# A fused attention block on one core: last projections a step earlier, gate scale four steps later, and an uneven last half block with its normalisation partly on TensorE

## The chip, the core and the metric

The kernel runs on one core of one Trainium2 chip. A core has five engines with queues of their own: TensorE (matmuls; PE in the profile, its weight loads PEld), VectorE (DVE), ScalarE (ACT), GpSimd (POOL), and SyncE (SP), which here only issues transfers. Sixteen DMA engines move the data. The metric is device microseconds for one execution; lower is better.

## The reference

One encoder layer over 1,024 tokens of width 1,024, in float32. One projection makes the inputs of two groups of eight heads of 64. Group A is attention in an 8 x 16 neighbourhood of a 16 x 64 token grid with a learned bias; group B is attention in a band of 128 tokens to each side with rotary positions and a learned sink. Each group's output is multiplied by SiLU of its gate columns; both are joined, projected, added to the scaled input and normalised by row.

```
h = x @ w_in
q_a, k_a, v_a, z_a, q_b, k_b, v_b, z_b = split(h)
y_a = neighborhood_attention(q_a, k_a, v_a, rel_bias)
y_b = windowed_gqa_with_sink(rotary(q_b), rotary(k_b), v_b, sink)
mixed = concat([y_a * silu(z_a), y_b * silu(z_b)])
x = layer_norm(alpha * x + mixed @ w_out) * gain + bias
```

## The kernel before

**Precision.** Large products are done as three float16 matmuls: each operand is split into a high and a low part (`xh`/`xl`, `wh`/`wl`), and high x high, high x low and low x high are added up in PSUM. So a 128-column slice of weights against 512 tokens takes 8 x 3 = 24 matmuls, and a whole projection 48.

**Stages.** First come the values, the scales and six projections. Then follows a loop over steps, written in an order by hand: `units` holds 128 attention units (64 of group B, then 64 of group A, 16 to a pair of heads). At step i, unit i's scores are made (`stage_qk`, L818 and L819, in one of four `s` banks of PSUM), DVE adds the bias and takes the row's extreme (L828), ACT takes the exponential (L844); one step later ACT and DVE split the probabilities into high and low halves (`stage_tr`, L854 and L855), which frees the bank, and SP issues the DMA that transposes them (L858). Every fourth step `stage_pv` (L883) multiplies a quad of four units, split and sent off some steps before, with the values, one unit after the other; quad q is done at step 9 + 4q up to q = 29. `stage_ot` (L903, L912) transposes finished heads and multiplies in the gate.

**Filling.** Between these, `pump_to` issues matmuls of the remaining fifteen projections: project k of `FILL` is spread evenly between `FILL_AT[k]` and `FILL_AT[k + 1]`, so the list sets how many fill matmuls (L398) each step gets. The last four projections are z2, k3, q3 and z3: a gate, the key and the query of the last pair of heads (units 112 to 127), and the last gate. From step 121 on the fill is output projection (L1031). A finished projection is taken out of PSUM by ACT and DVE (for q3 L274 and L280, in two halves of the tokens); group A's keys are also copied by POOL (L312). Weight splits, loads of bias (L786), values (L742) and output weights (L969) are put into queues for ACT, DVE, POOL and SP, and a step takes a few from each. What a step needs at once is forced out by `need`. All transfers but a few go through SP, in program order, so a transfer waits for those ahead of it.

**Gate scale.** `m_scale(0)` to `m_scale(7)` work out one scale for the gated outputs: a matmul (`z_sum`, L644), then thirteen small DVE operations (L648 to L694), one piece a step from step 2 on. Its results are read by `stage_ot`, first at step 21.

**The end.** `final` does the output projection in blocks of 128 tokens (t) and 512 columns (a), then `residual` (L1080, and statistics L1081) and `norm`. The last block's second half is done as two pieces of 256 columns, `out_mms(7, 1, ps, EO, c)`, so that the statistics of the first run under the matmuls of the second. `norm_last(7)` then normalises in three column ranges: two on DVE (256 and 608 columns), one on ACT and POOL (160), and stores each.

Of the kernel before, what the change touches and what calls it, by code (L numbers as in the profile page):

```python
# [7 lines left out]
F32 = mybir.dt.float32  # L8
# [4 lines left out]
AF = mybir.ActivationFunctionType  # L13
ALU = mybir.AluOpType

S = 1024
D = 1024
# [4 lines left out]
ALPHA = 2.0 ** 0.25  # L22
# [12 lines left out]
DSUM = (4, 7)  # L35
NR = 8
FILL = ORDER[NPRO:]
FILL_AT = [0, 8, 17, 25, 33, 41, 49, 57, 66, 74, 81, 89, 97, 105, 112, 121, 123.5, 126, 128, 131, 136]
ZTAG = {"z3": "zv", "zb3": "zc", "z2": "zs", "zb1": "zd", "zb2": "ze"}
X1AT = 4  # L40
Z3_END = 119
# [6 lines left out]
WO_POST = (7, 8)  # L48
WO_MAX = 72
EO = (4, 5, 6, 7, 0, 1, 2, 3)  # L50
WO_AT = [80, 84, 88, 92, 128, 129, 130, 131]
WO_LD = [18, 22, 26, 30, 36, 39, 42, 45, 48, 112, 116, 33, 130, 130]
WIN0 = (0, 8, 24, 40)
# [9 lines left out]
def hybrid_block(ctx, tc, xT, x, wt, wv, wo, bias, sink, gain, lbias, cos, sin, bmask, out):  # L63
    nc = tc.nc
# [10 lines left out]
    def bank(tag):  # L75
        bufs = {"pj": 2, "s": 4, "t": 2}[tag]
        return (ps1 if bufs == 1 else ps2).tile([128, 512], F32, tag=tag, name=f"ps_{tag}", bufs=bufs)
# [13 lines left out]
    for half in range(2):  # L91
        for k in range(KT):
            t = big_tile(f"x{half}{k}")
# [7 lines left out]
    identf = const.tile([128, 128], F32, name="identf")  # L101
# [328 lines left out]
    with ExitStack() as vctx:  # L430
# [5 lines left out]
        ps = bank("t")  # L436
# [140 lines left out]
        for i in range(8):  # L577
# [5 lines left out]
            ps = bank(tags[i])  # L583
# [434 lines left out]
    Q30 = LP + 3 + 4 * (len(units) // 4 - 2)  # L1018
    NU = len(units)
    def out_mms(t, a, ps, es, c=None):  # L1020
        w = 512 if c is None else 256
        o = 0 if c is None else 256 * c
        ts, cs = slice(128 * t, 128 * t + 128), slice(o, o + w)
        ps = ps[:, o:o + w]
        for e in es:
            n = WO_SEQ.index((e, a))
            if n in wo_ops:
                need(wo_ops[n], *m_ops.get(e, ()))
            woh, wol = wo_parts[n]
            for i, (lh, rh) in enumerate(((mh[e], woh), (mh[e], wol), (ml[e], woh))):  # L1030
                nc.tensor.matmul(ps, lh[:, ts], rh[:, cs],  # L1031
                                 start=(e == EO[0] and i == 0), stop=(e == EO[-1] and i == 2))
                yield
# [14 lines left out]
    def final():  # L1048
        actx.close()
        fp = ctx.enter_context(tc.tile_pool(name="fp", bufs=2, reuse_waits="tile"))  # L1050
        eps = fp.tile([128, 1], F32, name="eps", bufs=1)
        nc.vector.memset(eps, EPS)
        tiles["fp"] = fp
        for e in EO[4:]:
            m_alloc(e, fp)
        for n in range(8, 14):
            nc.gpsimd.tensor_scalar(wo_raw[n], wo_raw[n], wos, 1.0, op0=ALU.mult, op1=ALU.mult)
        for e in EO[4:]:
            m_split(e, slice(0, 512), nc.scalar.copy, nc.vector.tensor_sub)
            for n in (WO_SEQ.index((e, 0)), WO_SEQ.index((e, 1))):  # L1060
                wo_split(n)
        for e in EO[4:]:
            m_split(e, slice(512, S), nc.scalar.copy, nc.vector.tensor_sub)
        gb, bb = gain_tile[0], zslot("bb")
        nc.sync.dma_start(bb, lbias.partition_broadcast(128))
        xrs, stats = {}, {}

        def x_load(t):
            if t < 8:
                xrs[t] = fp.tile([128, D], F32, tag="xr", name="xr", bufs=NX)  # L1070
                nc.sync.dma_start(xrs[t], x[t])

        def residual(t, a, ps, c=None):
            if a == 0:
                stats[t] = fp.tile([128, 4, 6], F32, tag="stats", name="stats")
            for k in range(2) if t == 7 and c is None else (c,):
                w = 512 if k is None else 256
                o = 0 if k is None else 256 * k
                xv = xrs[t][:, 512 * a + o:512 * a + o + w]
                nc.vector.scalar_tensor_tensor(xv, ps[:, o:o + w], oinv, xv, op0=ALU.mult, op1=ALU.add)  # L1080
                nc.vector.bn_stats(stats[t][:, a if k is None else 2 * a + k, :], xv)  # L1081

        def row_stats(t):
            mv = fp.tile([128, 2], F32, tag="mv", name="mv")
            nc.vector.bn_aggr(mv, stats[t][:, :4 if t == 7 else 2, :])
            sd = fp.tile([128, 1], F32, tag="sd", name="sd")
            nc.scalar.activation(sd, mv[:, 1:2], AF.Sqrt, bias=eps, scale=ALPHA ** 2)
            return mv, sd

        def row_scale(mv, sd):  # L1090
            rstd = fp.tile([128, 1], F32, tag="rstd", name="rstd")
            nc.vector.reciprocal(rstd, sd)
            nc.vector.tensor_scalar_mul(rstd, rstd, ALPHA)
            nmr = fp.tile([128, 1], F32, tag="nmr", name="nmr")
            nc.vector.scalar_tensor_tensor(nmr, mv[:, 0:1], -1.0, rstd, op0=ALU.mult, op1=ALU.mult)
            return rstd, nmr

        def norm_last(t):
            ts = slice(128 * t, 128 * t + 128)
            xr = xrs[t]  # L1100
            mv, sd = row_stats(t)
            h0, h1, h2 = slice(0, 256), slice(256, 864), slice(864, 1024)
            nc.vector.scalar_tensor_tensor(xr[:, h0], xr[:, h0], mv[:, 0:1], gb[:, h0], op0=ALU.subtract, op1=ALU.mult)
            rstd, nmr = row_scale(mv, sd)
            nc.scalar.activation(xr[:, h2], xr[:, h2], AF.Identity, bias=nmr, scale=rstd)
            nc.vector.scalar_tensor_tensor(xr[:, h1], xr[:, h1], mv[:, 0:1], gb[:, h1], op0=ALU.subtract, op1=ALU.mult)
            nc.gpsimd.tensor_mul(xr[:, h2], xr[:, h2], gb[:, h2])
            nc.gpsimd.tensor_add(xr[:, h2], xr[:, h2], bb[:, h2])
            for h, q in ((h1, nc.sync), (h0, nc.scalar)):
                nc.vector.scalar_tensor_tensor(xr[:, h], xr[:, h], rstd, bb[:, h], op0=ALU.mult, op1=ALU.add)  # L1110
                q.dma_start(out[ts, h], xr[:, h])
            nc.sync.dma_start(out[ts, h2], xr[:, h2])

        def norm(t):
            ts = slice(128 * t, 128 * t + 128)
            xr = xrs[t]
            mv, sd = row_stats(t)
            h0, h1 = slice(0, 512), slice(512, 1024)
            nc.vector.scalar_tensor_tensor(xr[:, h0], xr[:, h0], mv[:, 0:1], gb[:, h0], op0=ALU.subtract, op1=ALU.mult)
            rstd, nmr = row_scale(mv, sd)  # L1120
            nc.scalar.activation(xr[:, h1], xr[:, h1], AF.Identity, bias=nmr, scale=rstd)  # L1121
            nc.vector.scalar_tensor_tensor(xr[:, h0], xr[:, h0], rstd, bb[:, h0], op0=ALU.mult, op1=ALU.add)
            nc.sync.dma_start(out[ts, h0], xr[:, h0])
            nc.gpsimd.tensor_mul(xr[:, h1], xr[:, h1], gb[:, h1])  # L1124
            nc.gpsimd.tensor_add(xr[:, h1], xr[:, h1], bb[:, h1])
            nc.sync.dma_start(out[ts, h1], xr[:, h1])

        for t in range(NX):
            x_load(t)
        def finish(t, a, ps):  # L1130
            residual(t, a, ps)
            halves.setdefault(t, set()).add(a)
            for n in range(normed[0], t + 1):
                if n < 7 and len(halves.get(n, ())) == 2:
                    norm(n)
                    x_load(n + NX)
                    normed[0] += 1

        halves, normed = {}, [0]
        for t, tag in ((0, "t"), (1, "t"), (2, "s")):  # L1140
            obank[t, 1] = bank(tag)
            list(out_mms(t, 1, obank[t, 1], EO[:4]))
        for e in EO[4:]:
            for t, a in sorted(obank):
                list(out_mms(t, a, obank[t, a], [e]))
                if e == EO[-1]:
                    finish(t, a, obank[t, a])
        tags = iter(("pj", "t", "pj", "t", "s", "s", "s", "s"))
        for t, a in ((3, 1), (4, 1), (5, 0), (5, 1), (6, 0), (6, 1)):
            ps = bank(next(tags))  # L1150
            list(out_mms(t, a, ps, EO))
            finish(t, a, ps)
        ps = bank(next(tags))
        list(out_mms(7, 0, ps, EO))
        residual(7, 0, ps)
        for c in range(2):
            ps = bank(next(tags) if c == 0 else "pj")
            list(out_mms(7, 1, ps, EO, c))
            residual(7, 1, ps, c)
        with tc.manual_schedule():  # L1160
            norm_last(7)
# [12 lines left out]
    for i in range(-LD, NU + LO):  # L1174
# [5 lines left out]
        per, h = divmod(i, 16)  # L1180
# [31 lines left out]
        q, m = divmod(i - LP - 3, 4)  # L1212
        if i >= Q30 + 2:
            q, m = (NU // 4 - 2, i - Q30 - 2) if i < Q30 + 4 else divmod(i - LP - 3, 4)
        elif i >= Q30:
            q, m = -1, 0
# [6 lines left out]
        if 0 <= i - LT < NU:  # L1223
            stage_tr(units[i - LT])
        early = pop("act", 1, 0)
        if 2 <= i < 10:
            m_scale(i - 2)
        if i == WO_MAX + 3:
            wo_turn()
        if WO_MAX + 4 <= i < WO_MAX + 7:  # L1230
# [94 lines left out]
```

## Time and profile before

| | |
|---|---|
| median of 3 runs | 450.46 us (450.2 to 450.88) |
| the profiled execution | 450.19 us |
| its span, first to last instruction | 448.4 us |
| mean granted TensorE clock | 0.994 of full speed |
| DMA | 83.86 MB, 187 GB/s on the mean |

The profile is of one execution. Busy times are sums over an engine's instructions; a matmul's end is modelled, so starts are the safer figure. A step of the loop is found in the timeline by its scores: the i-th instruction of L818 is step i. Step 9 starts at 138.98 us, step 110 at 329.98, step 113 at 335.60, step 121 at 349.62.

### The profile page before, as it was taken

The page shows a single profiled execution, that of the slowest core. Times are in us where ns is not written, and L with a number is a line of the kernel's source. Part 1 is how long each engine was busy: PE and PEld are TensorE (multiplying, and loading weights), DVE is VectorE, ACT ScalarE, POOL GpSimd, SP SyncE. Part 2 cuts the span into 40 slices and gives each one's busy share as a digit, 9 for nine tenths or more (in the row PEclk, how much of TensorE's full clock was granted, in tenths as well). Part 3 has the DMA queues.
Part 4 walks back from the last instruction along what each step waited for, and adds up shares of the span by engine and source line. Part 5 has one row for each costly group of instructions (what it writes and reads, how often), then busy time and mean ns, then how long its engine had stood idle before and what let it go on. Part 6 is the DMA issues. An engine that isn't in the chain of part 4 may idle for free.

```text
span 448.4 us, 9544 instructions
## 1 busy us (share of the span) xinstructions
PE 438.1 (98%) x3265; PEld 263.4 (59%) x3265; DVE 347.2 (77%) x860; ACT 303.4 (68%) x702; POOL 231.2 (52%) x246
## 2 busy tenths in 40 slices
PE   8999999999999999999999999999999999999992
PEld 8999974444445555565555655656555654444452
DVE  5787987929989797786898788887878847189954
ACT  5648649877488898798979887887778974012200
POOL 0003942564927848768507639755473646005741
PEclk9999999999999999999999999999999999999997
DMA  8898377977747999877898989979989989101711
GB/s 256 283 316 270 93 251 251 292 254 266 280 124 158 154 167 166 153 151 142 150 170 169 192 169 188 212 153 233 201 158 213 197 187 342 48 0 70 259 71 70
DMA packets 135280, 83.86 MB, mean 187 GB/s; under 512 B 101440, under 2 KB 113600, under 8 KB 134976
## 3 DMA queue, kind: packets, MB, share of 16 engines
q1 hardware_dynamic: 134800, 82.84, 75.3%
q8 instruction: 25, 0.41, 0.4%
q10 hardware_dynamic: 432, 0.43, 0.3%
q14 instruction: 23, 0.19, 0.1%
HBM read 52.83 MB, written 9.96 MB: 140 GB/s over the span
## 4 chain that ended last, share of the span: by engine, by line
PE 87%; DVE 4%; ACT 3%; DMA 3%; issue 1%; POOL 1%; DVEq 0%; POOLq 0%; ACTq 0%
PE ps_pj L398 40%; PE ps_s L1031 9%; PE ps_t L883 7%; PE ps_s L479 6%; PE ps_pj L1031 5%; PE ps_t L1031 5%; PE ps_s L818 4%; PE ps_s L819 3%; PE ps_pj L479 3%; PE ps_t L479 3%; DMA wos<-in_wo 2%; PE ps_t L903 1%; DVE sn L828 1%; ACT ps_s L844 1%; DMA xraw<-in_xT 1%
## 5 line engine op out<-in xcount | busy, mean ns | idle before, releaser
L398 PE MATMUL ps_pj<-xf,wh 128*128 128x512 f16 x672 | 202.2, 379 | 0.0
L398 PE MATMUL ps_pj<-xf,wl 128*128 128x512 f16 x336 | 127.5, 379 | 0.0
L398 PEld LDWEIGHTS <-wh 128*128 128x128 f16 x672 | 63.6, 98 | 59.7 <-issue 0.2
L844 ACT ACTIVATE ps_s<-sn,nm 128x385 f32<-128x385 f32 (+3 forms) x128 | 70.1, 548 | 27.1 <-DVE nm L828 25.9
L855 DVE SCALAR_TENSOR_TENSOR split<-ps_s,split 128x384 f16<-128x384 f32 (+2 forms) x128 | 65.6, 513 | 21.0 <-ACT split L854 20.2
L1031 PEld LDWEIGHTS <-m 128*128 128x128 f16 x408 | 39.6, 98 | 41.4
L854 ACT ACTIVATE split<-ps_s 128x384 f16<-128x384 f32 (+2 forms) x128 | 57.6, 450 | 2.5
L398 PEld LDWEIGHTS <-wl 128*128 128x128 f16 x336 | 32.8, 98 | 37.5
L205 POOL TENSOR_SCALAR wr<-wr,wsc 128x512 f32<-128x512 f32 x26 | 21.7, 836 | 41.6 <-ACT wh L200 36.0
L828 DVE CUSTOM_DVE_ANT_0 sn<-ps_s,bias,sg 128x264 f32<-128x264 f32 (+1 forms) x64 | 35.2, 549 | 10.3 <-PE ps_s L819 4.8
L828 DVE CUSTOM_DVE_ANT_0 sn<-ps_s,bm,nsk 128x384 f32<-128x384 f32 (+1 forms) x64 | 40.7, 636 | 1.5 <-PE ps_s L819 1.3
L1031 PE MATMUL ps_s<-wo,m 128*128 128x512 f16 (+1 forms) x192 | 40.7, 366 | 0.0
L818 PE MATMUL ps_s<-ks,qs 128*128 128x384 f16 (+4 forms) x128 | 39.3, 307 | 0.9 <-DVE qs L280 0.7
L819 PE MATMUL ps_s<-ks,qs 128*128 128x384 f16 (+4 forms) x128 | 39.2, 307 | 0.0
L883 PEld LDWEIGHTS <-tr 128*128 128x128 f16 (+1 forms) x1104 | 36.6, 98 | 2.2
L790 POOL TENSOR_SCALAR bias<-bias,rsg 128x552 f32<-128x552 f32 (+1 forms) x24 | 18.6, 776 | 36.4 <-DMA bias<-in_bias 33.0
L206 POOL TENSOR_TENSOR wl<-wr,wh 128x512 f16<-128x512 f32 x26 | 32.2, 1239 | 2.2
L1124 POOL TENSOR_TENSOR xr<-xr,gb 128x512 f32<-128x512 f32 x7 | 11.1, 1600 | 38.7 <-ACT xr L1121 38.7
L479 PE MATMUL ps_s<-wvh,x 128*128 128x320 f32 x128 | 29.9, 313 | 0.0
L312 POOL COPY ks<-ks 64x512 f16<-64x512 f16 x40 | 26.0, 660 | 4.7 <-DVE ks L282 1.8
L1031 PE MATMUL ps_pj<-wo,m 128*128 128x512 f16 (+1 forms) x120 | 26.5, 358 | 0.0
L527 POOL TENSOR_SCALAR xraw<-xraw,xsc 128x512 f32<-128x512 f32 x5 | 4.5, 903 | 39.5 <-ACT xf L525 39.5
(182 smaller groups left out, 827.1 us busy)
## 6 DMA issues: line engine op xcount, KB each, us to landing
xraw<-in_xT SPq DMA_DIRECT2D x31, 256.0 KB, 4.3
ws<-in_wt SPq DMA_DIRECT2D x15, 512.0 KB, 5.4
wr<-in_wt SPq DMA_DIRECT2D x26, 256.0 KB, 3.2
bias<-in_bias SPq DMA_DIRECT2D x16, 276.0 KB, 3.2
wor<-in_wo SPq DMA_DIRECT2D x16, 256.0 KB, 3.2
xr<-in_x SPq DMA_DIRECT2D x8, 512.0 KB, 8.5
out<-xr SPq DMA_DIRECT2D x14, 256.0 KB, 2.1
bias<-in_bias SPq DMA_DIRECT2D x8, 368.0 KB, 3.8
```

The lines of the kernel that those rows point to most:

```text
L206: nc.gpsimd.tensor_sub(l, raw, h)
L312: nc.gpsimd.tensor_copy(t[o, sl], t[a, sl])
L398: nc.tensor.matmul(ps, a[:, k % 4, :], mv, start=(k == 0 and i == 0), stop=(k == KT - 1 and i == 2))
L479: nc.tensor.matmul(ps[:, :320], lh[t // 4, k][:, ts], rh[k][:, cs], start=(k == 0 and i == 0), stop=(k == KT - 1 and i == 2))
L818: nc.tensor.matmul(ps[:, :m], q, sl[0], start=True, stop=False)
L819: nc.tensor.matmul(ps[:, :m], q, sl[1], start=False, stop=True)
L828: nc.vector.tensor_tensor_reduce(sn[:, :m], ps[:, :m], bias_t, sg[:, c:c + 1], init, op0=ALU.add, op1=ALU.min, accum_out=nm)
L844: nc.scalar.activation(pt[:, :m], sn[:, :m], AF.Exp, bias=nm, scale=-1.0, accum_out=sm[:, k:k + 1])
L854: nc.scalar.activation(hl[:, :m, 0, :c], src, AF.Copy, scale=PSCALE)
L855: nc.vector.scalar_tensor_tensor(hl[:, :m, 1, :c], src, PSCALE, hl[:, :m, 0, :c], op0=ALU.mult, op1=ALU.subtract)
L883: nc.tensor.matmul(ps[:, HD * m:HD * m + HD], a, b_, start=(i == 0), stop=(i == len(mms) - 1))
L1031: nc.tensor.matmul(ps, lh[:, ts], rh[:, cs], start=(e == EO[0] and i == 0), stop=(e == EO[-1] and i == 2))
```

## The change

It has three parts.

- `FILL_AT`: k3, q3 and z3 begin at steps 96, 104 and 111 instead of 97, 105 and 112. So z2 is spread over 7 steps instead of 8, z3 over 10 instead of 9; k3 and q3 keep 8 and 7.
- The pieces of `m_scale` run at steps 6 to 13 instead of 2 to 9.
- The last half block is cut into 384 and 128 columns instead of 256 and 256. Its normalisation is rewritten: DVE does the last 640 columns in two passes; for the first 384 it does only (x - mean) x alpha x gain, and TensorE adds the bias to that times 1/sd: an identity matmul of the bias, then a matmul with a diagonal matrix of 1/sd, both in float32 and into one bank, which ACT copies out. POOL is no longer used there. `ga` is gain x alpha, made by ACT once.

```diff
-FILL_AT = [0, 8, 17, 25, 33, 41, 49, 57, 66, 74, 81, 89, 97, 105, 112, 121, 123.5, 126, 128, 131, 136]
+FILL_AT = [0, 8, 17, 25, 33, 41, 49, 57, 66, 74, 81, 89, 96, 104, 111, 121, 123.5, 126, 128, 131, 136]
+LAST = ((0, 384), (384, 128))
+NPE = 384
...
     def out_mms(t, a, ps, es, c=None):
-        w = 512 if c is None else 256
-        o = 0 if c is None else 256 * c
+        o, w = (0, 512) if c is None else LAST[c]
...
+            pieces = ((a, 0, 512),)
+            if t == 7:
+                pieces = ((0, 0, 256), (1, 256, 256)) if c is None else ((2 + c,) + LAST[c],)
+            for n, o, w in pieces:
...
         def norm_last(t):
...
+            h0, h1 = slice(0, NPE), slice(NPE, D)
+            ga = fp.tile([128, D], F32, name="ga", bufs=1)
+            nc.scalar.mul(ga, gb, ALPHA)
             mv, sd = row_stats(t)
-            h0, h1, h2 = slice(0, 256), slice(256, 864), slice(864, 1024)
-            nc.vector.scalar_tensor_tensor(xr[:, h0], xr[:, h0], mv[:, 0:1], gb[:, h0], op0=ALU.subtract, op1=ALU.mult)
-            rstd, nmr = row_scale(mv, sd)
-            nc.scalar.activation(xr[:, h2], xr[:, h2], AF.Identity, bias=nmr, scale=rstd)
-            nc.vector.scalar_tensor_tensor(xr[:, h1], xr[:, h1], mv[:, 0:1], gb[:, h1], op0=ALU.subtract, op1=ALU.mult)
-            nc.gpsimd.tensor_mul(xr[:, h2], xr[:, h2], gb[:, h2])
-            nc.gpsimd.tensor_add(xr[:, h2], xr[:, h2], bb[:, h2])
-            for h, q in ((h1, nc.sync), (h0, nc.scalar)):
-                nc.vector.scalar_tensor_tensor(xr[:, h], xr[:, h], rstd, bb[:, h], op0=ALU.mult, op1=ALU.add)
-                q.dma_start(out[ts, h], xr[:, h])
-            nc.sync.dma_start(out[ts, h2], xr[:, h2])
+            ps = bank("t")
+            nc.tensor.matmul(ps[:, :NPE], identf, bb[:, h0], start=True, stop=False)
+            nc.vector.scalar_tensor_tensor(xr[:, h0], xr[:, h0], mv[:, 0:1], ga[:, h0], op0=ALU.subtract, op1=ALU.mult)
+            rstd = fp.tile([128, 1], F32, tag="rstd", name="rstd")
+            nc.vector.reciprocal(rstd, sd)
+            dg = fp.tile([128, 128], F32, name="dg", bufs=1)
+            nc.scalar.mul(dg, identf, rstd)
+            nc.tensor.matmul(ps[:, :NPE], dg, xr[:, h0], start=False, stop=True)
+            nc.vector.scalar_tensor_tensor(xr[:, h1], xr[:, h1], mv[:, 0:1], ga[:, h1], op0=ALU.subtract, op1=ALU.mult)
+            nc.vector.scalar_tensor_tensor(xr[:, h1], xr[:, h1], rstd, bb[:, h1], op0=ALU.mult, op1=ALU.add)
+            nc.sync.dma_start(out[ts, h1], xr[:, h1])
+            nc.scalar.copy(xr[:, h0], ps[:, :NPE])
+            nc.scalar.dma_start(out[ts, h0], xr[:, h0])
...
-        if 2 <= i < 10:
-            m_scale(i - 2)
+        if 6 <= i < 14:
+            m_scale(i - 6)
```

More of the change, by code (lines that the diff above doesn't have):

```diff
@@ L1075, in residual @@
                 stats[t] = fp.tile([128, 4, 6], F32, tag="stats", name="stats")
-            for k in range(2) if t == 7 and c is None else (c,):
-                w = 512 if k is None else 256
-                o = 0 if k is None else 256 * k
+            pieces = ((a, 0, 512),)
+            if t == 7:
+                pieces = ((0, 0, 256), (1, 256, 256)) if c is None else ((2 + c,) + LAST[c],)
+            for n, o, w in pieces:
                 xv = xrs[t][:, 512 * a + o:512 * a + o + w]
                 nc.vector.scalar_tensor_tensor(xv, ps[:, o:o + w], oinv, xv, op0=ALU.mult, op1=ALU.add)
-                nc.vector.bn_stats(stats[t][:, a if k is None else 2 * a + k, :], xv)
+                nc.vector.bn_stats(stats[t][:, n, :], xv)
         def row_stats(t):
```

## The prediction

> **What bounds the kernel now.** I read the page first, then the timeline of TensorE, then the timelines of the engines that end its waits, and last the tail after the last matmul.
>
> ```profile
> span 448.4 us, 9544 instructions
> PE 438.1 (98%) x3265; PEld 263.4 (59%) x3265; DVE 347.2 (77%) x860; ACT 303.4 (68%) x702; POOL 231.2 (52%) x246
> ```
>
> The profiled execution took 450.19 us, 1.8 us more than its span, and 0.27 us under the median of 450.46. TensorE is idle for some 10 us of the span: a little at the start, two short holes, and the tail. Every other engine costs time only where it makes one of these. The holes, from the timelines of the engines concerned (columns: start, us, engine and line):
>
> ```profile
> 136.90 0.34 DVE L682 TENSOR_TENSOR zg<-zg,wg 128x1 f32<-128x1 f32 x2
> 138.11 0.59 PE L398 MATMUL ps_pj<-xf,wh 128*128 128x512 f16 x2
> 138.38 0.55 DVE L855 SCALAR_TENSOR_TENSOR split<-ps_s,split 128x384 f16<-128x384 f32 x1
> 138.98 0.32 PE L818 MATMUL ps_s<-ks,qs 128*128 128x384 f16 x1 [0.28 <-DVE zg L684]
> ...
> 334.34 0.59 PE L398 MATMUL ps_pj<-xf,wh 128*128 128x512 f16 x2
> 334.86 0.68 DVE L280 SCALAR_TENSOR_TENSOR qs<-ps_pj,qs 64x512 f16<-64x512 f32 x1 [0.80 <-ACT qs L274]
> 335.60 0.30 PE L818 MATMUL ps_s<-ks,qs 128*128 128x288 f16 x1 [0.66 <-DVE qs L280]
> ...
> 414.25 5.18 PE ps_t L1031 x24
> ```
>
> A stream of 512-column matmuls starts one every 5.18/24 = 0.216 us (last row, from the chain of waits). At 138.11 two were issued, so the next could have started at 138.11 + 0.43 = 138.54; it started at 138.98: **0.44 us lost** at step 9, whose scores need the bank that unit 5's split (L855) frees at 138.93. DVE was late because the gate-scale pieces (L682 and others) stand between. At 334.34 likewise: 334.77 against 335.60, **0.83 us lost** at step 113, whose second-half query (L280) came late out of a projection that ended with step 111.
>
> **Edit 1, gate scale at steps 6 to 13.** One small matmul and thirteen DVE operations move four steps later; nothing is added. The split that releases step 9 then has four pieces fewer ahead of it; only the one at 136.90 (0.34) surely stands behind the last ACT wait, so the gain is 0.3 to 0.44; I take 0.4. The pieces land where DVE has more room:
>
> ```profile
> 127.50:139.00 11.50, 11.22 (x58) 5.43 (x57) 9.48 (x32) 10.34 (x24) 4.63 (x5) 1.00 0.43 89
> 139.00:155.00 16.00, 16.00 (x166) 9.37 (x166) 13.46 (x46) 14.18 (x37) 13.72 (x13) 1.00 0.84 156
> ```
>
> (Windows: length, then busy time of PE, PEld, DVE, ACT, POOL, clock, DMA.) DVE is 82% busy before 139 and 84% after, but after it TensorE has its probability products as well and waits for nobody in 16.00 us. Their cost there: nothing, or at worst the 0.34 of one piece. The result is first used at step 21.
>
> **Edit 2, last projections a step earlier.** The query of the last pair is then done a step before it is wanted, and the 0.83 us goes. What is late next? Nothing is removed from TensorE: z2's 48 matmuls run in seven steps, the last gate's in ten. At step 110 there are then 41 matmuls of q3 issued instead of 34, so step 110's scores come 7 x 0.216 - 0.44 = 1.07 us later than before; at step 121 the counts are equal, and TensorE would be 0.44 + 0.83 = 1.27 us early. No weights are loaded by these projections; their splits on ACT and POOL move along with them. The queue they are moved past is SP's, which issues the transposed probabilities, and it is full:
>
> ```profile
> 329.98 0.28 PE L818 MATMUL ps_s<-ks,qs 128*128 128x264 f16 x1
> ...
> 331.33 0.55 DVE L855 SCALAR_TENSOR_TENSOR split<-ps_s,split 128x384 f16<-128x384 f32 x1
> ...
> 330.67 2.56 SPq L858 DMA_TRANSPOSE tr<-split  x2
> 333.29 0.57 SPq L742 DMA_DIRECT2D va<-vwin  x1
> ...
> 336.52 1.22 SPq L858 DMA_TRANSPOSE tr<-split  x1
> 337.78 0.58 SPq L742 DMA_DIRECT2D va<-vwin  x1
> 338.78 0.33 SPq L786 DMA_DIRECT2D bias<-in_bias  x1
> ...
> 351.36 2.54 SPq L858 DMA_TRANSPOSE tr<-split  x2
> ...
> L858 SPq DMA_TRANSPOSE tr<-split x1: 1228/1228/1228, 352.7 to 352.7; - x1
> DMA to landing us min/median/max: 3.6/3.6/3.6
> DMA to landing us min/median/max: 2.9/3.6/3.8
> ...
> 355.63 1.22 PE L883 MATMUL ps_t<-va,tr 128*128 128x64 f16 x36
> ```
>
> Unit 109's transpose is the second of the two at 330.67, so it starts at 332.0, a moment after its split (331.33 + 0.55 = 331.88). From there to 352.7 SP issues without a pause but for some 0.4 us before 338.78 and 0.1 before 336.52. Unit 119's, issued at 352.7, lands 3.6 later, at 356.3 (the next row is of the three issued from 352.7 on: 2.9 to 3.8). TensorE wants it with the 28th of the 36 products that begin at 355.63, at 355.63 + 27 x 0.029 = 356.4 (0.029 = (1.22 - 0.19)/35). So **behind the stall that goes stands a cover of 0.1 to 0.2 us**: unless SP is earlier too, TensorE waits there for what it has gained.
>
> Is SP earlier? Unit 109's split stands on DVE behind the bias of unit 110, which needs step 110's scores. Before, the split ended 331.88 - 329.98 = 1.90 after them; with the query's split out of the way it could be 1.4 (matmul pair 0.39, bias 0.42, split 0.55, hand-over 0.05). With the scores 1.07 later, the transpose is 0.55 to 1.05 later; I take 0.65, near the low end, since the query's pieces do move away. SP can win back its 0.4 of pauses: unit 119 is issued about 0.25 later, and TensorE gets on 0.1 us later than before. Ends: 0.6 earlier (all pauses won back, landing in 3.0 instead of 3.6, as the quickest nearby) to 0.9 later (nothing won back). **Front, both edits: +0.1 us, from -0.6 to +0.9.**
>
> **Edit 3, the tail.**
>
> ```profile
> 429.83 0.75 DVE L1080 SCALAR_TENSOR_TENSOR xr<-ps_s,oinv,xr 128x512 f32<-128x512 f32 x1 [2.90 <-PE ps_s L1031]
> 430.62 0.69 DVE L1081 BATCH_NORM_STATS2 stats<-xr 128x6 f32<-128x512 f32 x1
> ...
> 437.59 2.63 PE ps_pj L1031 x24
> 440.25 0.48 DVE L1080 SCALAR_TENSOR_TENSOR xr<-ps_pj,oinv,xr 128x256 f32<-128x256 f32 x1 [1.67 <-PE ps_pj L1031]
> 440.77 0.43 DVE L1081 BATCH_NORM_STATS2 stats<-xr 128x6 f32<-128x256 f32 x1
> 441.23 0.26 DVE L1085 BATCH_NORM_AGGREGATE mv<-stats 128x2 f32<-128x24 f32 x1
> 441.53 0.49 DVE L1103 SCALAR_TENSOR_TENSOR xr<-xr,mv,gb 128x256 f32<-128x256 f32 x1
> 441.59 0.29 ACT L1087 ACTIVATE sd<-mv,eps 128x1 f32<-128x1 f32 x1 [7.89 <-DVE mv L1085]
> 441.93 0.16 DVE L1092 RECIPROCAL rstd<-sd 128x1 f32<-128x1 f32 x1
> 442.39 0.84 DVE L1106 SCALAR_TENSOR_TENSOR xr<-xr,mv,gb 128x608 f32<-128x608 f32 x1
> 442.55 0.52 ACT L1105 ACTIVATE xr<-xr,nmr,rstd 128x160 f32<-128x160 f32 x1 [0.67 <-DVE nmr L1095]
> 443.27 1.71 DVE L1110 SCALAR_TENSOR_TENSOR xr<-xr,rstd,bb 128x608 f32<-128x608 f32 x2
> 445.01 0.35 ACTq L1111 DMA_DIRECT2D out<-xr  x1
> ...
> 349.87 0.60 PE L903 MATMUL ps_t<-identf,on 128*128 128x128 f32 x4
> 442.80:445.00 2.20, 0.00 (x0) 0.00 (x0) 2.14 (x3) 0.27 (x1) 1.47 (x2) 0.50 0.00 0
> L854 ACT ACTIVATE split<-ps_s 128x384 f16<-128x384 f32 x80 | 38.5, 482 | 1.4
> ```
>
> The matmuls do the same columns, so the last one ends as before. The 384-column piece leaves 24 x 0.055 = 1.3 us (half of 2.63/24 each) in which DVE does its residual and statistics, 0.62 + 0.56 by interpolation between 256 and 512 columns: just hidden, and 0.1 if not. The last 128 columns cost 0.35 + 0.30 instead of 0.48 + 0.43: 0.26 earlier. The first subtraction is 384 wide, 0.13 longer, so the reciprocal starts at 441.80 instead of 441.93. DVE then drops two small operations and does 640 columns twice at 0.88 (0.84 x 640/608): 441.99 to 443.8, and SP's store is issued at 443.9. The other 384 columns go by ACT's diagonal (0.5, nearest row the 160-wide 0.52; 442.0 to 442.5), a float32 matmul d, an ACT copy of 0.48 and a store: issued at 442.55 + d + 0.53. That path ends last when d is over 0.8. The gain multiple (two of 0.8 us for 1,024 columns) and the bias matmul lie in ACT's 7.89 us of idle time and in TensorE's empty time; uncovered, the bias matmul would delay d by at most 0.1.
>
> No row shows a full float32 product. The nearest: float32 transposes start (0.60 - 0.27)/3 = 0.11 us apart for 128 columns, so 384 columns once through cost 0.33. The kernel itself makes a fine product out of three matmuls; three or four of these make 1.0 to 1.3, and at the clock of 0.50 that is granted from 442.8 on, 2.0 to 2.6. I take d = 1.3, as part may run at full clock: store at 444.4 instead of 445.01. [...]
>
> The clock is 0.50 from 2.5 us after the last full-rate matmul. [...]
>
> The last store is 192 KB instead of 128, behind 320 KB: 0.1. **Tail: -0.5 us; from -1.0** (d of 0.33: SP's 443.9 is then last) **to +0.8** (d of 2.6). Sum: +0.1 - 0.5 = -0.4 us: 449.8 for the profiled execution, **450.0 by the median**; this case's own range is 449.2 to 451.0.
>
> **The rivals.**
> *SP does not hold.* Bias and split follow the scores faster, or transposes land in 3.0 us, and the front keeps its 1.2: 450.46 - 1.2 - 0.8 (d near 1.0) = 448.5. For it: landing times here vary. Against it: unit 109 cannot leave before its later scores.
> [...]
> *The stall at 113 only moves.* The query is still split late and TensorE waits as before. With SP as the bound this changes nothing: 450.0 again.
>
> **How the numbers follow.** A measurement of this kernel can tell about 0.2% (0.9 us) from no change. Forecast, the moved stall included: 0.60, of which 0.10 lies below 449.6 and 0.02 above 451.4. SP does not hold: 0.32, nearly all faster (0.30). Cold matmul: 0.08, of which 0.06 slower. Faster 0.40, same 0.52, slower 0.08. The range is 448.2 to 451.0, to take in most of the first rival.
>
> **What would show it.** Right: no wait at step 9 or 113; unit 109's transpose issued 0.5 to 1 us later than 332.0 although TensorE gained 0.4 before; new waits of L883 on transposes in the quads at steps 121 and 125, together over 1 us; last store near 444.4 less the front. Wrong: L883 never waits and the last matmul starts over a microsecond earlier; or the copy out of PSUM starts after 445.

## The result, and the profile after

The changed kernel took **454.1 us** by the median of ten runs (450.73 to 456.3), the kernel before 450.78 beside it (449.98 to 451.26): ratio 1.0066, 95% interval 1.0049 to 1.0084. It is slower by 0.7%, and outside the predicted 448.2 to 451.0. The profile first taken of it was of the quickest of its ten executions (450.73 us); a later profile of the same code (run e15) took 454.29 us, near the median, and is the one read below as "the changed kernel".

The head of the page, first of the quick execution, then of the one near the median:

```profile
span 448.9 us, 9547 instructions
PE 440.5 (98%) x3269; PEld 263.6 (59%) x3269; DVE 347.7 (77%) x857; ACT 304.9 (68%) x704; POOL 230.0 (51%) x244
...
span 452.5 us, 9547 instructions
PE 441.5 (98%) x3269; PEld 263.6 (58%) x3269; DVE 344.8 (76%) x857; ACT 304.5 (67%) x704; POOL 229.6 (51%) x244
```

TensorE's work is the same within 1 us; 3.6 us lie between the spans. Where they went is in TensorE's timeline, in the quad of products (L885, L883 before) that takes units 116 to 119, at step 125. In the changed kernel:

```profile
355.40 1.03 PE L1032 MATMUL ps_pj<-wo,m 128*128 128x512 f16 x4
356.59 0.69 PE L885 MATMUL ps_t<-va,tr 128*128 128x64 f16 x18
357.96 0.44 PE L885 MATMUL ps_t<-va,tr 96*128 96x64 f16 x9 [0.68 <-DMA tr<-split]
360.00 0.66 PE L885 MATMUL ps_t<-va,tr 96*128 96x64 f16 x9 [1.60 <-DMA tr<-split]
360.47 1.90 PE L1032 MATMUL ps_pj<-wo,m 128*128 128x512 f16 x4
```

Before, the 36 products ran without a hole (1.22 us). Here the third unit's nine (unit 118) could have started at 356.59 + 18 x 0.029 = 357.11 and started at 357.96: 0.85 lost. The last nine could have started at 357.96 + 9 x 0.029 = 358.22 and started at 360.00: 1.78 lost. Both waits end with the landing of a transpose. Then four 512-column matmuls take 1.90 where the same four took 1.03 five microseconds earlier. The windows (length, busy time and count of PE, PEld, DVE, ACT, POOL, granted clock, DMA) say why:

```profile
357.10:360.40 3.30, 1.02 (x24) 0.78 (x20) 1.45 (x4) 1.81 (x6) 0.72 (x1) 0.86 1.40 170
360.40:363.40 3.00, 3.00 (x14) 1.31 (x12) 0.46 (x3) 0.13 (x1) 0.00 (x0) 0.58 0.79 155
363.40:367.00 3.60, 3.60 (x22) 1.77 (x21) 2.28 (x9) 3.08 (x8) 0.31 (x1) 1.00 0.69 135
```

TensorE stood for 2.3 of 3.3 us; after that it works without a pause, at a granted clock of 0.58: 3.0 x (1 - 0.58) = 1.3 us more. So in this execution one late transpose costs twice. In the quick execution the same quad lost 0.4 and the clock stayed at 1.00.

Unit 119's transpose is the late one. Its issue on SP and landing, in the kernel before and in the changed one, and the DMA view around it (the row of the queue of instructions in a stretch of the kernel before and in one of the changed kernel, then the GB/s row of the changed kernel's next stretch):

```profile
L858 SPq DMA_TRANSPOSE tr<-split x1: 1228/1228/1228, 352.7 to 352.7; - x1
DMA to landing us min/median/max: 3.6/3.6/3.6
...
L860 SPq DMA_TRANSPOSE tr<-split x1: 1228/1228/1228, 354.9 to 354.9; - x1
DMA to landing us min/median/max: 5.1/5.1/5.1
...
q8 instruction: 1, 0.02, 9.0%
...
q8 instruction: 1, 0.02, 7.3%
...
GB/s 0 0 0 0 0 0 0 0 0 0 0 0 0 6 6 6 6 6 13 6 13 6 13 6 13 6 13 6 13 6 13 6 19 115 250 288 301 275 251 232
```

It is issued 2.2 us later and takes 1.5 us more. The stretches are 356.2 to 357.0 before and 357.5 to 358.4 after: in each, one packet of 16 KB comes on the queue of instructions (at 356.51 and 357.91). Such a packet is called a fetch below. Before, unit 119 had landed at 356.23, ahead of it. After, it was still in flight, and from 358.4 to 359.7 the DMA engines move next to nothing (last row: 1.6 us in 40 slices); then it lands, at 359.95.

The times of both profiled executions are 450.19 and 454.29, 4.1 apart. Adding TensorE's losses, after less before: gate scale at step 9 -0.3 (0.13 instead of 0.44) and at step 17 +0.8; step 113 -0.1; a wait at 130 us +0.6, which e3 also shows (0.64) though its edit lies 300 us later, and which is therefore not the change's; the start -0.5; the quad at step 121 (units 112 to 115) +0.4; this quad +2.6; the half clock +1.3; the tail -0.9. The sum is 3.9.

### The profile page after: what moved, and what is told of

It reads as the page before. It is cut to its first block, busy times and chain, and to the rows that moved or that the text cites. A ratio compares the mean times of both kernels' runs of the same rounds, so it can differ in the third digit from the quotient of the medians.

```text
span 448.9 us, 9547 instructions
## 1 busy us (share of the span) xinstructions
PE 440.5 (98%) x3269; PEld 263.6 (59%) x3269; DVE 347.7 (77%) x857; ACT 304.9 (68%) x704; POOL 230.0 (51%) x244
## 4 chain that ended last, share of the span: by engine, by line
PE 87%; DVE 4%; DMA 4%; ACT 3%; issue 1%; ACTq 0%; DVEq 0%
PE ps_pj L400 41%; PE ps_s L1032 9%; PE ps_t L885 7%; PE ps_s L481 6%; PE ps_t L1032 5%; PE ps_pj L1032 5%; PE ps_s L820 3%; PE ps_s L821 3%; PE ps_pj L481 3%; PE ps_t L481 3%; DMA wos<-in_wo 2%; PE ps_t L905 2%; DVE sn L830 1%; DVE split L857 1%; DMA tr<-split 1%
## 5 line engine op out<-in xcount | busy, mean ns | idle before, releaser
L1032 PEld LDWEIGHTS <-m 128*128 128x128 f16 x408 | 38.7, 98 | 42.3
L1032 PE MATMUL ps_s<-wo,m 128*128 128x512 f16 (+1 forms) x192 | 42.0, 372 | 0.0
L885 PEld LDWEIGHTS <-tr 128*128 128x128 f16 (+1 forms) x1104 | 36.7, 98 | 2.5 <-DMA tr<-split 0.3
L208 POOL TENSOR_TENSOR wl<-wr,wh 128x512 f16<-128x512 f32 x26 | 32.2, 1239 | 2.2
L1089 ACT ACTIVATE sd<-mv,eps 128x1 f32<-128x1 f32 x8 | 2.4, 295 | 43.2 <-DVE mv L1087 40.9
L1032 PE MATMUL ps_pj<-wo,m 128*128 128x512 f16 (+1 forms) x120 | 25.2, 347 | 0.0
```

The lines of the kernel that those rows point to most:

```text
L208: nc.gpsimd.tensor_sub(l, raw, h)
L885: nc.tensor.matmul(ps[:, HD * m:HD * m + HD], a, b_, start=(i == 0), stop=(i == len(mms) - 1))
L1032: nc.tensor.matmul(ps, lh[:, ts], rh[:, cs], start=(e == EO[0] and i == 0), stop=(e == EO[-1] and i == 2))
```

## The experiments

**One part at a time.** The gate scale alone; the three bounds alone; the tail alone; and the whole again.

```
e1  before, with   if 6 <= i < 14: m_scale(i - 6)
e2  before, with   FILL_AT = [..., 89, 96, 104, 111, 121, ...]
e3  after, with    FILL_AT = [..., 89, 97, 105, 112, 121, ...]  and  if 2 <= i < 10: m_scale(i - 2)
e4  after, unchanged
```

> The kernel before with the gate scale alone moved to steps 6 to 13. Theory A (the new wait of the scores on DVE's split at step 17, 0.82 us in the profile after, is what this part adds, against 0.44 lost before at step 9): slower by 0.2 to 0.6 us, 451.0 to 451.4. Theory B (the 3.3 us are this part's, by a DVE backlog that varies between executions): 453 to 454.5. As predicted: 0.4 us faster, 450.4.

> The kernel before with FILL_AT alone changed. Theory A (SP is the bound and the last products wait for their transposes): within 0.5 us of before, 450.3 to 451.3. Theory B (the 3.3 us come from here, the late transposes being later still in most executions): 453 to 454.5. No bound by SP: 450.0.

> The kernel before with the 384 and 128 columns and the new last normalisation alone. As predicted: 0.5 us faster, 450.3; by the profile after (last store issued 5.1 us after the last full-size matmul instead of 4.8): 0 to 0.3 slower, 451. Theory B (the 3.3 us are the tail's, its float32 matmuls running at half clock or the new tiles changing what final waits for): 453 to 454.5.

> The changed kernel once more, for a profile of an execution of the common time. Its median should be near 454.1 and its executions spread from 450.7 to 456 as before. If the profile is of a slow one, the 3.3 us stand in it as waits of TensorE in one place (start, step 17, quads 28 to 31, or final), or as a longer tail.

Beside a kernel before of 450.88: e1 **451.3** (ratio 1.0001, 0.9983 to 1.0019), e2 **453.96** (1.0053, 1.0028 to 1.0079), e3 **450.1** (0.9976, 0.9958 to 0.9994), e4 **452.8** (1.0052, 1.0033 to 1.0070). The loss is in the three bounds; the tail alone beats both kernels. E4 is the same code as the first measurement and came 1.3 us under it: medians of one kernel can differ by that much here.

The gate scale did not give its 0.4: its wait went from step 9 to step 17. DVE and then TensorE of the changed kernel, the same in e1 (0.82 at 152.7):

```profile
147.08 1.06 DVE L689 TENSOR_TENSOR zg<-zg,vg 128x1 f32<-128x1 f32 x1
150.69 0.77 DVE L696 TENSOR_TENSOR zcol<-vscb,msc 128x1 f32<-128x1 f32 x2
152.58 0.55 DVE L857 SCALAR_TENSOR_TENSOR split<-ps_s,split 128x384 f16<-128x384 f32 x1
...
152.16 0.38 PE L400 MATMUL ps_pj<-xf,wl 128*128 128x512 f16 x1
153.18 0.32 PE L820 MATMUL ps_s<-ks,qs 128*128 128x384 f16 x1 [0.65 <-DVE split L857]
```

Step 17's scores could have started at 152.16 + 0.22 = 152.38 and started at 153.18, behind a split that DVE gave at 153.13. One-column pieces of the gate scale stand before it on DVE: one took 1.06, a pair 0.77, where the pair at step 9 had taken 0.34. The trace shows with what the long ones end: that of 1.06 ends at 148.14, where GpSimd's product L284 ends at 148.12, and the long one of the pair (0.70) at 151.40, where GpSimd's L208 ends at 151.38. In the kernel before, in the changed one and in e1, a one-column product of the gate scale takes 0.15 to 0.17 us; the eleven that took longer all ended 0.01 to 0.02 us after such a two-operand operation of GpSimd. That GpSimd holds them up is how this reads; no run was made to try it.

**The fetch.** Is the packet of instructions the cause of the long landing, or does it only stand beside it? The fetch can be moved without touching anything near it (though all the other fetches move with it): the warm-up at the start of the kernel has 27 matmuls of 128 columns, and other shapes fill about the same time with other numbers of instructions.

```
e5  the three bounds, and the warm-up as 7 matmuls of 512 columns (40 instructions fewer)
e6  before, and the warm-up as 36 matmuls of 96 columns (18 instructions more)
```

> The kernel before with the projections' steps changed (as in the second run of the first set), and the 27 warm-up matmuls of 128 columns at the start made 7 of 512: the same time on TensorE there, 40 instructions fewer. Theory A (the instruction fetch decides): the DMA queue of instructions brings TensorE's code, 16 KB each 10 to 11 us near the end, at a fixed place in TensorE's stream; transposes that land after it are about 2 us late. With 40 instructions fewer ahead the fetch that was seen at 358.65 comes about 1.6 us later in TensorE's work, the transpose of unit 119 lands in 3.6 us instead of 5.2, TensorE's wait for it is under 0.7 us instead of 2.4, the clock of 0.50 after it is gone: 451.5 us, from 450.8 to 452.3. Theory B (SP's lateness alone, the landing being long for another reason): unit 119 lands in over 5 us as before and the time stays at 454.0.

> The kernel before with nothing changed but the warm-up at the start: 36 matmuls of 96 columns instead of 27 of 128, 18 instructions more. Theory A: the fetch comes 0.7 us earlier than 356.51, at 355.8, ahead of the landing of unit 119 (356.23), which becomes 5 us instead of 3.6; TensorE waits 1.3 to 2 us in that quad, with some loss to the clock in part of the executions: 452.5 us, from 452.0 to 454. Theory B: no difference from before, 450.9.

Beside 450.64: e5 **452.41** (1.0040, 1.0027 to 1.0054), e6 **452.05** (1.0026, 1.0013 to 1.0039). E6 first: TensorE's timeline, the landing of units 118 and 119, the fetch in a window from 354.5 to 356, and the clock afterwards.

```profile
355.46 0.95 PE L883 MATMUL ps_t<-va,tr 128*128 128x64 f16 x27
358.17 0.43 PE L883 MATMUL ps_t<-va,tr 96*128 96x64 f16 x9 [1.75 <-DMA tr<-split]
...
DMA to landing us min/median/max: 4.1/4.6/5.0
...
q8 instruction: 1, 0.02, 7.2%
...
358.80:362.10 3.30, 3.30 (x12) 1.44 (x10) 1.48 (x5) 0.98 (x3) 0.00 (x0) 0.50 0.70 135
```

Nothing is changed but nine more, narrower matmuls at 1 to 4 us, and 355 us later the kernel before has the very wait of the changed one, 358.17 - (355.46 + 27 x 0.029) = 1.9 us, and the clock of 0.50 behind it. The fetch came at 355.04, 1.5 us earlier where 0.7 was worked out, and unit 119, issued at 353.12, took 5.0 us. The issue itself was 0.45 later than before, and the quad began 0.17 earlier: some 0.4 of the 1.9 are SP's lateness, 1.5 the longer landing. E5 is the same in the other direction:

```profile
350.96 1.03 PE L883 MATMUL ps_t<-va,tr 96*128 96x64 f16 x27
352.89 0.44 PE L883 MATMUL ps_t<-va,tr 128*128 128x64 f16 x9 [0.90 <-DMA tr<-split]
...
357.43 1.19 PE L883 MATMUL ps_t<-va,tr 128*128 128x64 f16 x27
358.86 0.43 PE L883 MATMUL ps_t<-va,tr 96*128 96x64 f16 x9 [0.23 <-DMA tr<-split]
...
DMA to landing us min/median/max: 3.6/3.6/3.6
```

With the fetch at 360.71, unit 119 lands in 3.6 us again and TensorE loses 0.6 there (2.4 in e2), with no half clock. The time misses its range by 0.1, for a reason in the first two rows: the fetch before this one moved too, to 347.9, and makes the quad before wait for 1.1. So the fetch decides which transpose is late, and the bounds decide whether there is cover for it.

All 17 profiles, each of one execution, agree: in the nine where the fetch came 1.9 to 3.25 us after the issue of unit 119, that transpose took 4.9 to 5.6 us to land; in the eight where it came 3.45 us or more after, 2.9 to 3.8.

**SP's queue, and which bound.**

```
e7  the three bounds, and WO_LD = [..., 48, 123, 124, 33, 130, 130]   (112, 116 before)
e8  before, with FILL_AT = [..., 89, 97, 105, 111, 121, ...]
```

> The kernel before with the projections' steps changed, and two loads of the output weight that SP issues at steps 112 and 116 (0.57 us each) put at steps 123 and 124, behind the transpose of unit 119. If SP's full queue carries the lateness (theories A and B both): unit 119 is issued 0.8 to 1.1 us earlier, ahead of the fetch, and lands in 3.6 us; TensorE's wait goes from 2.4 us to under 0.3: 451.2 us, from 450.5 to 452.0. If the loss has nothing to do with SP (theory C: the later scores and bank frees of the other steps): 454.0 as without.

> The kernel before with one number changed: the last query ends with step 111 (112 before), the other two bounds stay at 97 and 105. The scores of step 110 then come behind 40 of its matmuls instead of 34, 1.3 us later, against 36 if only the other two bounds were moved. If this bound makes SP late: unit 109's transpose 1.2 to 2 us later, unit 119 behind the fetch, the wait at step 113 still there with 0.7: 454.0 us, from 452.5 to 455. If the earlier start of the other projections makes the loss: 450.9.

E7 **451.53** (1.0024, 1.0008 to 1.0039): two issues of 0.57 us taken out of SP's queue give back 2.4 of the 3.1 us of e2 by the medians, 1.3 of 2.4 by the ratios, whose intervals overlap. E8 **453.3** (1.0053, 1.0022 to 1.0085): the end of the last query alone makes nearly all of the loss, though four of its twelve executions lie at 450.8 to 450.9 and the others from 452.7 up. Both times are as expected. The mechanism expected of e7 is not in its profile, which is of one of its two longest executions (453.34): the fetch came at 356.55, unit 119 took 5.6 to land, and TensorE waited 2.5 for it after all. The cover is wider there, not sure.

**Putting the parts together.** The tail with SP's queue relieved; the whole change with it; the tail with it and the last query ending two steps earlier; the tail with a fetch a little later.

```
e9   e3 with WO_LD 123, 124           e10  after with WO_LD 123, 124
e11  e9 with FILL_AT = [..., 97, 105, 110, 121, ...]
e12  e3 with the warm-up as 20 matmuls of 172 columns (14 instructions fewer)
```

> The new tail with the old projection and gate-scale steps, and the two loads of the output weight moved from steps 112 and 116 to 123 and 124, behind the transpose of unit 119. If executions of one kernel differ because that transpose lands just ahead of the instruction fetch or just behind it: unit 119 is issued 0.7 to 1.1 us earlier, always lands ahead, and the slow executions go: median 449.8 us, highest under 451.3 (the tail alone had 450.1 and 452.1). If the scatter has another cause: median 450.1 and highest over 452 as without the move.

> The changed kernel, all three edits, with the two loads of the output weight moved from steps 112 and 116 to 123 and 124. If SP's lateness ahead of the fetch is what the whole change lost: the projections with free SP had 451.5, the tail takes off 0.8 and the gate scale adds at most 0.4, which gives 451.0 us, from 450.4 to 451.7. If something that the three edits make together costs the time: 453 or more.

> The new tail, the loads moved, the gate scale and two of the projection bounds as before, and the last query ending with step 110 instead of 112. Theory of the stall at step 113: with a bound of 111 the DVE half of the query's split waits for the second ACT copy, which stands behind an exponential; with 110 both stand one unit earlier, and the stall of 0.8 us goes. Theory of SP: all 48 of its matmuls are issued by step 110 instead of 34, 3 us of scores later, of which 1.1 are won back by the moved loads; unit 119 lands behind the fetch and TensorE waits 1.5 to 2.5 us: 451.2 us, from 450.4 to 452.5. If SP has room for it: 449.1 us.

> The new tail alone, and the 27 warm-up matmuls of 128 columns made 20 of 172: 14 instructions fewer on TensorE, so that the instruction fetch near the end comes some 0.6 to 1.2 us later against the transposes, without reaching the quad before. If the scatter of the tail alone (449.33 to 452.13) comes from that fetch: unit 119 lands in 3.6 us always, median 449.7 us, highest under 451.2. If not: 450.1 and the same scatter.

E9 **450.46** (0.9992, 0.9981 to 1.0003), highest 451.28: the highest came down as expected, the median did not. TensorE has a new wait of 0.6 us, for an output weight:

```profile
371.27 1.24 PE L1032 MATMUL ps_s<-wo,m 128*128 128x512 f16 x5
372.97 0.59 PE L1032 MATMUL ps_s<-wo,m 128*128 128x512 f16 x2 [0.46 <-POOL wo L999]
```

The moved loads are not what it waits for; they landed at 360.22 and 362.38. GpSimd makes this weight behind a load that was not moved: it is issued at 367.01 and lands at 370.95, where e3 has 366.55 and 370.25.

E10 **452.24** (1.0035, 1.0018 to 1.0052) misses its range by 0.5: it wins back part of the loss. Its profile (451.51) shows what SP's relief was to do: unit 119 is issued at 353.82 instead of 354.87, ahead of the fetch, lands in 3.8, and TensorE waits 0.2 there; but 0.9 of a new wait stands in the next quad. E11 **453.74** (1.0070, 1.0047 to 1.0094) is worse than expected by 2.5, though both mechanisms show:

```profile
337.97 0.38 PE L400 MATMUL ps_pj<-xf,wh 128*128 128x512 f16 x1
338.19 0.29 PE L820 MATMUL ps_s<-ks,qs 128*128 128x288 f16 x1
...
357.11 0.69 PE L885 MATMUL ps_t<-va,tr 128*128 128x64 f16 x18
358.11 0.43 PE L885 MATMUL ps_t<-va,tr 96*128 96x64 f16 x9 [0.31 <-DMA tr<-split]
360.25 0.44 PE L885 MATMUL ps_t<-va,tr 96*128 96x64 f16 x9 [1.71 <-DMA tr<-split]
```

Step 113's scores follow their matmul by 0.22: the stall is gone for the first time. And the quad loses 2.3. Its profile has another 1.3 at 125 us, far from any change, and 0.6 at 354.8; at both TensorE waits for a copy of a gate on DVE (L361), and why that was late was not followed. E12 **449.87** (0.9979, 0.9963 to 0.9995; 449.19 to 451.22) is near what was expected, and cannot be told from e3 by its interval; the two are the best versions found. That its fetch is later is not shown: the profile has it at 357.44, e3's at 357.56.

**Do the parts add up?**

```
e13  after with m_scale at steps 2 to 9        e14  after with the old tail        e15  after, unchanged
```

> The changed kernel with the gate scale back at steps 2 to 9: the projections' steps and the tail. If the parts add up (projections +3.1 by medians, tail -0.8, gate scale +0.5 by the traces): 453.0 us, 0.5 under the whole change run beside it. If gate scale and projections make more together than each alone: 452 or less, over 1 us under the whole change.

> The changed kernel with the old tail: the projections' steps and the gate scale. If the parts add up: 454.3 us, 0.8 over the whole change run beside it. If the new tail's gain is not there once the front is late: the same as the whole change.

> The changed kernel once more, beside the two above. By its two measurements: 453.4 us, from 452.8 to 454.1.

Beside 450.9: e13 **453.32** (1.0046, 1.0030 to 1.0061), e14 **453.45** (1.0050, 1.0027 to 1.0074), e15 **454.3** (1.0058, 1.0038 to 1.0078). Taking the gate scale back gains 1.0 where 0.5 was expected; taking the tail back should have cost 0.8 and did not; e15 lies 0.2 over its range. With intervals of 0.3 to 0.5% these differences prove nothing beyond e1 to e3. If gate scale and bounds cost more together than alone, e13 was to be 452 or less, and it was not; whether the tail keeps its gain behind a late front stays open.

## Why the prediction was wrong, point by point

**Bound of the front: right mechanism.** SP was said to be full, with almost no cover for unit 119 behind the stall, and TensorE to wait there. That is where the time went; the sizes were wrong, in four terms. Against the forecast of -0.4 the traces have +3.9. Of the 4.3 between them, 1.7 are a gain that did not come (-1.27 at steps 9 and 113, measured +0.4), 1.6 the waits for transposes (3.0 instead of some 1.4), and 1.3 the half clock; the tail gives back 0.4, and 0.1 is the start and the wait at 130 us.

**Edit 1, -0.4: wrong sign.** Measured +0.5 in the traces (-0.3 at step 9, +0.8 at step 17), 0 to +0.4 by the runs of e1. There was room: in the kernel before, the splits that free the banks for steps 15, 16 and 17 end 0.95, 1.13 and 0.87 us ahead of TensorE. The price of the pieces was wrong, and they used it up (0.17, 0.08 and none in the changed kernel). The worst case of 0.34 was a pair at step 9, while a pair took 0.77 later on and a single one 1.06. The two windows of the prediction held a warning in the column that was not read: GpSimd, beside which these pieces turned out long, is busy for 4.63 of 11.50 us before 139 and for 13.72 of 16.00 after. With the 0.4 gone the lateness of step 110's scores was 7 x 0.216 = 1.5 us and more, not 1.07.

**The stall at 113, which "goes": it moved.** That was the last rival, and it held: 0.83 before, 0.73 after. ACT, DVE and TensorE of the changed kernel:

```profile
334.48 0.58 ACT L276 ACTIVATE qs<-ps_pj 64x512 f16<-64x512 f32 x1
334.96 0.51 ACT L846 ACTIVATE ps_s<-sn,nm 128x288 f32<-128x288 f32 x1
335.61 0.59 ACT L276 ACTIVATE qs<-ps_pj 64x512 f16<-64x512 f32 x1
...
336.24 0.68 DVE L282 SCALAR_TENSOR_TENSOR qs<-ps_pj,qs 64x512 f16<-64x512 f32 x1 [0.94 <-ACT qs L276]
...
336.04 0.38 PE L400 MATMUL ps_pj<-xf,wl 128*128 128x512 f16 x1
336.98 0.30 PE L820 MATMUL ps_s<-ks,qs 128*128 128x288 f16 x1 [0.56 <-DVE qs L282]
```

The query is projected a step earlier, but of its two ACT copies the second now stands behind an exponential, and DVE's first split of that half starts only after the second copy (before, it started after the first). Why it waits for both was not tried apart; that the stall goes when all of it is done one step earlier still, e11 shows.

**SP wins back 0.4 and lands in 3.6, at the quickest 3.0: the step that failed.** Unit 109's transpose was to be 0.65 later and unit 119's 0.25. In the changed kernel they are at 334.02 and 354.87, 2.0 and 2.2 later than before: nothing was won back. In the quick execution they are 2.5 and 1.6 later, and SP did win back about 1. The two differ by one issue on SP, that of unit 114, which stands beside a fetch (at 344.84 and 345.56; first the changed kernel, then the quick execution):

```profile
345.01 2.62 SPq L860 DMA_TRANSPOSE tr<-split  x1
...
345.51 1.51 SPq L860 DMA_TRANSPOSE tr<-split  x1
```

Elsewhere such an issue takes 1.2 in the median. In the kernel before, the 14 transposes issued within 1 us of a fetch took 1.6 to issue in the median, the other 114 took 1.2.

The second half of the step, the landing, was taken as a constant with an end on the good side only. The kernel before itself had shown 5.9 and 5.3 us for two transposes (issued at 343.04 and 344.98), and a fetch of instructions at 346.28 between their issue and their landing. Over the 122 transposes that the kernel before issues between 140 and 366 us, the median is 4.1 us for the 34 with such a fetch between 0.5 us before the issue and the landing, and 3.05 for the 88 without (90% of these under 3.8); in the changed kernel 4.0 and 3.0. A long flight is likelier to meet a fetch, but that alone does not make the difference: counted by fetches within 2 us after the issue, it is 4.0 for 17 and 3.1 for 105. Unit 119 was 0.3 us ahead of one. In the changed kernel it lands in 5.1. Both quads named for new waits have them, 0.4 at step 121 and 2.6 at step 125: together 3.0, over 1 us as the prediction's sign had it.

**The clock in the front: left out.** The prediction used the drop of the clock for the tail and did not ask what a wait of 2 us can do in the middle: 1.3 us in the execution near the median, nothing in others (below).

**Edit 3, -0.5: right sign, too small.** -0.8 by medians (0.9976). The tail of e3, TensorE, DVE, ACT, SP, then windows (columns as above):

```profile
439.21 1.50 PE L1032 MATMUL ps_pj<-wo,m 128*128 128x128 f16 x24
440.55 0.86 PE L1108 MATMUL ps_t<-bb,identf 128*128 128x384 f32 x2
442.95 0.91 PE L1114 MATMUL ps_t<-xr,dg 128*128 128x384 f32 x2 [1.53 <-ACT dg L1113]
...
443.28 0.88 DVE L1116 SCALAR_TENSOR_TENSOR xr<-xr,rstd,bb 128x640 f32<-128x640 f32 x1
442.49 0.40 ACT L1113 ACTIVATE dg<-identf,rstd 128x128 f32<-128x128 f32 x1 [0.37 <-DVE rstd L1111]
443.94 0.48 ACT L1118 COPY xr<-ps_t 128x384 f32<-128x384 f32 x1 [1.05 <-PE ps_t L1114]
444.45 0.35 ACTq L1119 DMA_DIRECT2D out<-xr  x1
444.19 0.33 SPq L1117 DMA_DIRECT2D out<-xr  x1
442.70:443.90 1.20, 0.91 (x2) 0.30 (x2) 1.17 (x2) 0.20 (x1) 0.00 (x0) 1.00 0.00 0
446.00:448.00 2.00, 0.00 (x0) 0.00 (x0) 0.00 (x0) 0.00 (x0) 0.00 (x0) 0.50 0.20 76
```

The mis-sized term is d, taken as 1.3: from 442.95 to the copy at 443.94 it is 0.96 with 0.03 of hand-over, all at clock 1.00, where the kernel before had 0.50 from 442.8 on; here it drops at 445.9. The bias matmul and the product lie between; whether they held the clock was not tried apart. The trace has the product as two matmuls, 0.91 us busy; three or four times 0.33 was the prediction's estimate, and no run shows it. The diagonal took 0.40 instead of 0.5. The last projection ends 0.5 later than before (440.71 against 440.22), so the last store, at 444.45, is 443.96 on the clock of before: 1.05 earlier than 445.01 and 0.4 under the forecast of 444.4. The paths end 0.26 apart, ACT's last, as forecast. The 0.1 for the larger last store was an estimate without a row: in the quick execution 192 KB landed 2.5 us after their issue, before 128 KB in 2.2. The cold matmul, given a chance of 0.08, did not happen: the product ran at 1.00; nor did "SP does not hold". That the tail came out better than forecast is no merit of the sum: 1.3 was a choice between its own 1.0 and 2.6.

## What to carry to other kernels

A transfer's time to land is a distribution (in the kernel before, 2.4 to 5.9 us for one kind of transpose between 140 and 366 us): where a step's cover is a few tenths, look up the longest landings of the same transfer in the trace and what they had in common, before one of them is taken as the price. A short operation has a price for each place (0.15 to 1.06 us here for a one-column product): ask which other engines are busy where it is moved to. If the wait behind a removed stall is on the one full queue, moving work earlier ahead of it can make the loss larger than the stall (here waits of 3.0 us for a stall of 0.83). And a wait of 2 us on TensorE is to be priced with the half clock that can follow it (1.3 us more in the changed kernel; it followed in four of the nine profiles that lose as much).

## What the runs showed of the hardware

**Transposes in flight beside a fetch land later.** On the queue of instructions whose packets are 16 KB, 25 came between 14 and 420 us; between two of them the trace has 255 matmuls and weight loads in the mean (194 to 299), and fewer of these ahead move the packet later (e5: 360.71, where e2 has 358.65), more move it earlier (e6: 355.04, before 356.51). In the kernel before, a transpose beside one took 1 us more to land in the median (4.1 against 3.05), the longest 2.9 more (5.9). A second queue of instructions, with packets of 8 KB, shows less: the 18 transposes of the kernel before that have one of these alone beside them land in 3.2 in the median. What in the fetch holds the transposes, whose own packets are 256 bytes, no run here shows.

**The clock can drop after a wait of some 2 us.** Waits of 1.9 us (e6) and 0.85 + 1.78 us (the changed kernel) were followed by a clock of 0.50 for 3.41 us, from 358.81 and 359.50 on: 2.4 to 2.6 us after the wait began, in e6 0.6 after TensorE was at work again, in the changed kernel 0.5 before. A wait of this size does not always do it: of the nine profiles that lose 1.9 us or more in this quad, e2, e6, e14 and e15 have the drop, and e4, e7, e8, e11 and e13 keep 1.00 throughout. What decides is not shown.
